# A hybrid decoder trunk on one core: the attention outputs are turned inside the next job, and the plan dates combined rows later

## The chip, the core and the metric

The kernel runs on one core of one Trainium2 chip. A core has TensorE (matrix multiplies, called PE in the profile; its weight loads are PEld), VectorE (DVE), ScalarE (ACT), GpSimd (POOL) and SyncE (SP, which here only issues transfers). TensorE writes to PSUM, which has eight banks; the other engines copy results from there to SBUF. The metric is the device time of one execution in microseconds (us); less is better.

## The reference

Two layers of a decoder trunk over one sequence of 2048 positions, width 1024. Each layer computes

```
h = rmsnorm(x); proj = h @ w_in
o_mla  = softmax attention, 6 heads, q/k of 96, v of 64
o_diff = 4 heads: p = softmax(s0) - lam * softmax(s1); o = rmsnorm(p @ v)
o_rw   = RWKV-7 recurrence, 6 heads of 64
x = x + concat(o_mla, o_diff, o_rw) * silu(gate) @ w_out
```

and a final RMSNorm closes the trunk. Both attentions are causal. The second is called the difference attention below: its weights are the difference of two softmaxes, so two rows of exponentials are combined into one before the values are applied. All is float32.

## The kernel before

**Stages.** In each of the two layers the input projections and the RWKV recurrence come first (phase A), then both attentions side by side, then the output projection (`outp`). The first attention, `mla`, starts as soon as the projections are done, the difference attention, `diff`, when the recurrence is done; `outp` waits for the flag `diff` and, tile by tile, for the flag `mla`.

**Jobs.** An attention works through jobs of one head and 256 queries (two blocks of 128 queries, `qi` 0 and 1); `g` counts them from 0 to 7, and a job with a larger `g` has more keys, up to 2048. `mla` has 48 jobs a layer and `diff` 32. A score chain makes the rows of a job: matmuls of queries and keys into PSUM (line 1128), a pass of VectorE that masks, keeps a running extreme in `mx` and empties the bank (L1131), and one exponential of ScalarE on each 1024 columns (L1139). In `diff` this is done twice, into tiles `row` and `tmp`, and then `row + cf * tmp` is formed in pieces of 512 columns (`CPART`), each either on VectorE (one instruction, L1429) or on GpSimd (two, L1431 and L1432). A value chain, in the function `weighted` (lines 1052 to 1087), then turns the rows: TensorE transposes up to four blocks of 128 columns into one bank (L1064), ScalarE or VectorE copies the bank back over the row (L1066), matmuls with the values add up the output (L1074), the output is copied to `ob` (L1082), and `ob` is turned back (L1086). What follows is the finish of a job: a multiplication by the reciprocal of the softmax sum into `ot` (L1323, L1475), in `diff` also a norm (ScalarE L1480, VectorE and GpSimd L272 and L273, GpSimd L1483), and a transfer to `omt` in DRAM (L1324, L1485).

**The order.** Python generators, one for each chain, are interleaved by `weave` on a clock of planned times, `clk`. A chain yields the time from which it can go on; `weave` takes the chain that is ready, with a handicap for each chain (`BIAS_A`, `BIAS_D`, `BIAS_M`, `BIAS_O`). When none is ready the planned clock moves on to the earliest. The order in which the chains emit matmuls and transposes is the order of TensorE's instructions on the chip, which are run strictly in that order: a plan that dates something too early puts an instruction into the queue that then waits, with all behind it. The time at which a tile of a row is ready is kept in `row.done`, one number for each 1024 columns. A combination in `diff` sets it from `clk.best`, which chooses the engine from two linear costs and reserves that engine:

```
eng, t = clk.best(max(ready, clk.now), V=65 + 1.04 * n, P=PX + 3.25 * n)   # PX = -700
rr[0].done[c0 // 1024] = max(rr[0].done[c0 // 1024], t)
```

**Limits on running ahead.** The score chain may be `JA` = 4 jobs ahead of `done["n"]`, which the value chain counts up when a job is finished, and it needs free row tiles: 8 of 1024 columns in `mla`, 9 in `diff` with 4 of `tmp`. A row tile is free again when the value matmuls have read it (`row.read`).

Of the kernel before, what the change touches and what calls it, by code (L numbers as in the profile page):

```python
# [15 lines left out]
ALU = mybir.AluOpType  # L16
# [7 lines left out]
NT = S // 128  # L24
# [5 lines left out]
MH, MN, MR, MV = 6, 64, 32, 64  # L30
MQ = MN + MR
QR, KVR = 256, 128
DH, DD, DV = 4, 32, 64
# [20 lines left out]
DROWS, DTMP = 9, 4  # L54
JA = 4
PX = -700
HOP = 100.0
LOAD = 2500.0
VDB = 2
# [27 lines left out]
class Clock:  # L87
# [22 lines left out]
    def fit(self, t, eng, ns):  # L110

        i = self.taken[eng] = [x for x in self.taken.get(eng, []) if x[1] > self.now]
        t += HOP
        for s_, e in i:
# [5 lines left out]
    def run(self, t, eng, ns):  # L120

        t = self.fit(t, eng, ns)
        self.taken[eng] = sorted(self.taken[eng] + [(t, t + ns)])
        return t + ns + HOP

# [65 lines left out]
def trunk(tc, a, out):  # L191
    nc = tc.nc
    V, A, P, T, Q = nc.vector, nc.scalar, nc.gpsimd, nc.tensor, nc.sync
# [5 lines left out]
    def mk(p, shape, tag, dt=F32, bufs=None):  # L199
        return p.tile(list(shape), dt, name=tag, tag=tag, bufs=bufs)  # L200
# [70 lines left out]
    def rstd_of(dst, ss, scale, eps):  # L271
        V.tensor_scalar(dst, ss, scale, eps, ALU.mult, ALU.add)  # L272
        P.tensor_tensor(dst, dst, mhalf.to_broadcast(list(dst.shape)), ALU.pow)  # L273
# [20 lines left out]
    def phase_a(l, rq_t, near, far, flags):  # L294
# [380 lines left out]
        def rwkv_inv(u, cks):  # L675
# [10 lines left out]
            for s in range(1, SB - 1):  # L686
# [4 lines left out]
                V.tensor_tensor(w[:, 0:s, s + 1:SB], w[:, 0:s, s + 1:SB], t, ALU.add)  # L691
                te = clk.run(clk.run(te, "V", 65 + IPAD + 1.04 * n * m) - HOP, "V", 65 + IPAD + 1.04 * n * m) - HOP
                if s % 2 == 0:
# [355 lines left out]
        return list(zip([run_chain(), chunk_chain(), prep_chain(), out_chain(), later_chain(), proj_chain()], BIAS_A))  # L1049


    def weighted(rows, vget, g, p):


        copied = 0.0
        for c_ in range(g // 2 + 1):
            for qi, row in enumerate(rows):
                n = min(4, 2 * g + qi + 1 - 4 * c_)
                if n <= 0:
                    continue  # L1060
                yield from banks.wait(att, 1, lambda: row.done[c_ // 2])
                tp, b = banks.get(att, [128, 512])
                for k in range(n):
                    T.transpose(tp[:, k * 128:(k + 1) * 128], row.at(512 * c_ + 128 * k, 128), ident)  # L1064
                eng, t = clk.best(clk.pe(109 * n), A=50 + 0.84 * 128 * n, V=65 + 1.04 * 128 * n)
                (V.tensor_copy if eng == "V" else A.copy)(row.at(512 * c_, 128 * n), tp[:, 0:128 * n])  # L1066
                copied = max(copied, banks.give(b, t))
                yield clk.now
        yield from banks.wait(att, 1, lambda: copied)
        o, bo = banks.get(att, [128, 128])  # L1070
        for kb in range(2 * g + 2):
            for qi, row in enumerate(rows):
                if kb <= 2 * g + qi:
                    T.matmul(o[HEADS[qi]], vget(kb), row.at(kb * 128, 128), start=(kb == 0), stop=(kb == 2 * g + qi))  # L1074
                    clk.pe(108)
        clk.pe(250)
        for row in rows:
            for h in range(len(row.tiles)):
                row.read(h)
        ob = mk(p, [128, 128], "ob", bufs=2)  # L1080
        eng, t = clk.best(clk.now, A=158, V=198)
        (V.tensor_copy if eng == "V" else A.copy)(ob, o)  # L1082
        banks.give(bo, t)
        yield from banks.wait(att, 1, lambda: t)
        ps, b = banks.get(att, [128, 2, 64])
        T.transpose(ps.rearrange("p a b -> p (a b)"), ob, ident)  # L1086
        clk.pe(109)
        return ps, b
# [53 lines left out]
    def mla(l, rq_t, side, flags):  # L1142
# [3 lines left out]
        jobs, done = [], dict(n=0)  # L1146
# [164 lines left out]
                    jobs.append((hd, g, rows, lsum, vts))  # L1311

        def value_chain():
            for n in range(MH * NT // 2):
                yield lambda: len(jobs) > n
                hd, g, rows, lsum, vts = jobs[n]
                li = mk(tp_, [128, 2], "li")
                if g >= 4:
                    V.tensor_tensor(lsum[:, :, 0], lsum[:, :, 0], lsum[:, :, 1], ALU.add)
                V.reciprocal(li, lsum[:, :, 0])  # L1320
                ps, b = yield from weighted(rows, lambda kb: vts[kb // 4][:, kb % 4, hd % 2], g, tp_)
                t = mk(tp_, [128, 2, 64], "ot", bufs=4)
                V.tensor_tensor(t, ps, li.unsqueeze(2).to_broadcast([128, 2, 64]), ALU.mult)  # L1323
                Q.dma_start(out=sc["omt"][g * 256:(g + 1) * 256, hd * MV:(hd + 1) * MV].rearrange("(q p) c -> p q c", p=128),  # L1324
                            in_=t)
                done["n"] = flags["mla"] = n + 1
                yield banks.give(b, clk.run(clk.now, "V", 200))
            st.close()

        return list(zip([value_chain(), score_chain()], BIAS_M))  # L1330

    def diff(l, side, flags):
# [3 lines left out]
        jobs, done = [], dict(n=0)  # L1336
# [61 lines left out]
        def scores(h, g, qt, kts):  # L1398
            nonlocal dist
            rows = []  # L1400
            lsum = mk(tp_, [128, 2, 2, 2], "dls", bufs=JA + 2)
            for qi in range(2):
                i = 2 * g + qi
                nk = 128 * (i + 1)
                rr = []
                now, dist = dist, distances((i + 1) % NT, l + h == 0 and i + 1 < NT)
                yield now[1]
                for m in range(2):
                    def passes(c_, n):
                        return [(qt[:, m, qi * 128:qi * 128 + 128], kts[c_][:, m, 0:n])]  # L1410

                    def sub(c_, n, nc_):
                        return now[0][c_ // 2][:, 512 * (c_ % 2):512 * (c_ % 2) + n]

                    rr.append((yield from attend_qk(new[m], tp_, DSN, i, passes, sub, SLOPES[h], lsum[:, m, qi])))
                if nk > 1024:
                    V.tensor_tensor(lsum[:, :, qi, 0], lsum[:, :, qi, 0], lsum[:, :, qi, 1], ALU.add)
                cf = mk(tp_, [128, 1], "cf", bufs=4)
                V.reciprocal(cf, lsum[:, 1, qi, 0:1])
                V.scalar_tensor_tensor(cf, cf, nlam[:, 0:1], lsum[:, 0, qi, 0:1], ALU.mult, ALU.mult)  # L1420
                ready = clk.run(rr[1].done[-1], "V", 210)
                for k in range(len(rr[0].tiles)):
                    rr[0].done[k] = 0.0
                for c0 in range(0, nk, CPART):
                    n = min(nk - c0, CPART)
                    p, q = rr[0].at(c0, n), rr[1].at(c0, n)
                    eng, t = clk.best(max(ready, clk.now), V=65 + 1.04 * n, P=PX + 3.25 * n)
                    if eng == "V":
                        V.scalar_tensor_tensor(p, q, cf[:, 0:1], p, ALU.mult, ALU.add)  # L1429
                    else:  # L1430
                        P.tensor_scalar(q, q, cf[:, 0:1], 1.0, ALU.mult, ALU.mult)  # L1431
                        P.tensor_tensor(p, p, q, ALU.add)  # L1432
                    rr[0].done[c0 // 1024] = max(rr[0].done[c0 // 1024], t)
                for k in range(len(rr[1].tiles)):
                    rr[1].read(k)
                rows.append(rr[0])
            return rows, lsum
# [27 lines left out]
                    jobs.append((h, g, rows, lsum, vts))  # L1465

        def value_chain():
            for n in range(DH * NT // 2):
                yield lambda: len(jobs) > n
                h, g, rows, lsum, vts = jobs[n]  # L1470
                li = mk(tp_, [128, 2], "dli")
                V.reciprocal(li, lsum[:, 0, :, 0])
                ps, b = yield from weighted(rows, lambda kb: vts[kb // 4][:, kb % 4], g, tp_)
                t = mk(tp_, [128, 2, 64], "ot", bufs=4)
                V.tensor_tensor(t, ps, li.unsqueeze(2).to_broadcast([128, 2, 64]), ALU.mult)  # L1475
                free = banks.give(b, clk.run(clk.now, "V", 200))
                r = mk(tp_, [128, 2], "r", bufs=4)
                for qi in range(2):
                    sq = mk(tp_, [128, DV], "sq")
                    A.activation(sq, t[:, qi], AF.Square, accum_out=r[:, qi:qi + 1])  # L1480
                clk.run(free, "A", 480)
                rstd_of(r, r, 1.0 / DV, SUB_EPS)
                P.tensor_tensor(t, t, r.unsqueeze(2).to_broadcast([128, 2, 64]), ALU.mult)  # L1483
                c0 = MH * MV + h * DV
                Q.dma_start(out=sc["omt"][g * 256:(g + 1) * 256, c0:c0 + DV].rearrange("(q p) c -> p q c", p=128), in_=t)  # L1485
                done["n"] = n + 1
                yield free
            st.close()
            flags["diff"] = 1

# [97 lines left out]
    with tc.manual_schedule(engines={mybir.EngineType.PE}):  # L1588
        for l in range(L):
            near, far = "left", "right"  # L1590
            flags = dict(near=0, far=0, diff=0, mla=0)
# [24 lines left out]
```

## Time and profile before

| | us |
|---|---|
| time, median of 3 runs | 4140.12 (4137.6 to 4142.48) |
| the profiled execution | 4140.24 |
| its span, first to last instruction | 4138.5 |
| first attention stage with both attentions | about 1180 to 1870 |
| second one | about 3250 to 3910 |

The profile page gives the busy time of each engine. Matmuls are pipelined, so that a busy TensorE isn't one at its peak. A view of groups gives for each line its count, busy time, mean duration, and behind the second bar the idle time of the engine just before the group's instructions with what ended it. A view of waits lists who waited for what, in total, how often, and the longest. The timeline shows single stretches; behind a row, in brackets, is the idle time before it and what ended it. The granted clock of TensorE has two levels in these records: 1.00 is 2.4 GHz and 0.50 is 1.2 GHz.

### The profile page before, as it was taken

The page shows a single profiled execution, that of the slowest core. Times are in us where ns is not written, and L with a number is a line of the kernel's source. Part 1 is how long each engine was busy: PE and PEld are TensorE (multiplying, and loading weights), DVE is VectorE, ACT ScalarE, POOL GpSimd, SP SyncE. Part 2 cuts the span into 40 slices and gives each one's busy share as a digit, 9 for nine tenths or more (in the row PEclk, how much of TensorE's full clock was granted, in tenths as well). Part 3 has the DMA queues.
Part 4 walks back from the last instruction along what each step waited for, and adds up shares of the span by engine and source line. Part 5 has one row for each costly group of instructions (what it writes and reads, how often), then busy time and mean ns, then how long its engine had stood idle before and what let it go on. Part 6 is the DMA issues. An engine that isn't in the chain of part 4 may idle for free. (4 is left out here: it accounts for less than half of the span.)

```text
span 4138.5 us, 76536 instructions
## 1 busy us (share of the span) xinstructions
PE 3634.2 (88%) x27232; PEld 2927.9 (71%) x27232; DVE 2777.0 (67%) x7443; ACT 1915.8 (46%) x4507; POOL 1447.4 (35%) x1684
## 2 busy tenths in 40 slices
PE   6989989898877888989999899998988789888699
PEld 5766767676666777777776676676766677777577
DVE  3775667756767888983237766677667678888633
ACT  3444344443456656751044444444434566666511
POOL 3434344443223334421044443444422243344211
PEclk9999999999989989999999999999989899999899
DMA  4533444344465554626434444343444555445254
GB/s 113 137 98 99 106 110 123 87 108 121 123 181 175 160 155 143 179 91 212 141 102 124 109 109 111 88 129 85 110 107 121 148 159 165 132 141 164 88 178 138
DMA packets 681630, 534.69 MB, mean 129 GB/s; under 512 B 233344, under 2 KB 585120, under 8 KB 681248
## 3 DMA queue, kind: packets, MB, share of 16 engines
q1 hardware_dynamic: 636704, 506.20, 44.1%
q10 hardware_dynamic: 40448, 11.02, 1.3%
q0 software_dynamic: 4096, 12.59, 0.9%
q8 instruction: 215, 3.52, 0.4%
q14 instruction: 167, 1.37, 0.1%
HBM read 417.43 MB, written 112.21 MB: 128 GB/s over the span
## 5 line engine op out<-in xcount | busy, mean ns | idle before, releaser
L441 PE MATMUL b<-h,wh 128*128 128x512 f32 x3584 | 1207.7, 412 | 51.9 <-DVE xk L470 15.8
L397 POOL TENSOR_TENSOR wl<-raw,wh 128x512 fp32r<-128x512 f32 x440 | 607.2, 1383 | 706.8 <-ACT wh L396 611.9
L441 PEld LDWEIGHTS b<-h,wh 128*128 128x128 f32 x3584 | 678.5, 193 | 220.9 <-DVE xk L470 18.8
L441 PE MATMUL b<-h,wl 128*128 128x512 f32 x1760 | 719.6, 409 | 2.6 <-POOL wl L397 2.5
L1139 ACT ACTIVATE row<-row,mx 128x1024 f32<-128x1024 f32 (+6 forms) x480 | 428.8, 895 | 245.0 <-DVE mx L1131 228.9
L396 ACT CAST wh<-raw 128x512 fp32r<-128x512 f32 x448 | 273.3, 613 | 505.8 <-PE b L441 310.6
L1064 PE MATMUL b<-ident,row 128*128 128x128 f32 x2720 | 389.9, 292 | 129.1 <-DVE row L1429 54.7
L1064 PEld LDWEIGHTS b<-ident,row 128*128 128x128 f32 x2720 | 329.7, 150 | 174.1 <-DVE row L1429 33.5
L441 PEld LDWEIGHTS b<-h,wl 128*128 128x128 f32 x1760 | 338.7, 192 | 79.4 <-POOL wl L397 5.8
L1128 PE MATMUL b<-k,q 128*128 128x512 f32 (+3 forms) x1440 | 369.3, 386 | 25.0 <-DVE mx L1131 16.5
L1128 PEld LDWEIGHTS b<-k,q 128*128 128x128 f32 x1440 | 252.0, 196 | 76.9 <-DVE mx L1131 23.7
L689 DVE TENSOR_TENSOR am<-w 48x30 f32<-48x30 f32 (+14 forms) x480 | 220.8, 460 | 88.6 <-DMA w<-linv 76.1
L1066 ACT COPY row<-b 128x512 f32<-128x512 f32 (+3 forms) x434 | 204.0, 505 | 111.3 <-PE b L1064 106.1
L1066 DVE COPY row<-b 128x512 f32<-128x512 f32 (+3 forms) x366 | 219.5, 621 | 49.6 <-PE b L1064 46.4
L1431 POOL TENSOR_SCALAR tmp<-tmp,cf 128x512 f32<-128x512 f32 (+2 forms) x144 | 118.4, 827 | 366.9 <-DVE cf L1420 238.1
L691 DVE TENSOR_TENSOR w<-w,am 48x30 f32<-48x30 f32 (+14 forms) x480 | 235.8, 491 | 12.9
L1074 PE MATMUL b<-row,v 128*64 128x128 f32 x3264 | 227.9, 287 | 13.2 <-ACT row L1066 7.7
L1074 PEld LDWEIGHTS b<-row,v 128*64 128x64 f32 x3264 | 202.1, 144 | 36.7 <-ACT row L1066 11.9
L1128 PE MATMUL b<-dk,dq 128*128 128x512 f32 (+3 forms) x640 | 200.6, 401 | 26.8 <-DVE mx L1131 12.3
L1564 PE MATMUL b<-wo,m 128*128 128x512 f32 x512 | 206.0, 402 | 0.0
L1139 ACT ACTIVATE tmp<-tmp,mx 128x1024 f32<-128x1024 f32 (+2 forms) x192 | 171.3, 894 | 73.9 <-DVE mx L1131 73.7
L1566 PE MATMUL b<-wo,m 128*128 128x512 f32 x512 | 203.5, 397 | 0.0
(279 smaller groups left out, 6629.7 us busy)
## 6 DMA issues: line engine op xcount, KB each, us to landing
raw<-in_w_in_dram SPq DMA_DIRECT2D x432, 256.0 KB
lq<-lat SPq DMA_DIRECT2D x192, 256.0 KB
d<-dist SPq DMA_DIRECT2D x70, 512.0 KB
lk<-lat SPq DMA_DIRECT2D x48, 512.0 KB
x<-in_x_dram SPq DMA_DIRECT2D x32, 512.0 KB
gat<-st SPq DMA_DIRECT2D x64, 256.0 KB
dk<-dqk SPq DMA_DIRECT2D x128, 128.0 KB
dq<-dqk SPq DMA_DIRECT2D x256, 64.0 KB
```

The lines of the kernel that those rows point to most:

```text
L396: A.copy(hi[:, :, 0:m], raw[:, :, 0:m])
L397: P.tensor_tensor(lo[:, :, 0:m], raw[:, :, 0:m], hi[:, :, 0:m].bitcast(F32), ALU.subtract)
L441: T.matmul(ps[0:w], x[k // 4][:, k % 4, 0:w], y, start=(k == 0 and i == 0), stop=(k == KD - 1 and i == len(ops) - 1))
L689: V.tensor_tensor(t, w[:, 0:s, s:s + 1].to_broadcast([48, n, m]), w[:, s:s + 1, s + 1:SB].to_broadcast([48, n, m]), ALU.mult)
L691: V.tensor_tensor(w[:, 0:s, s + 1:SB], w[:, 0:s, s + 1:SB], t, ALU.add)
L1064: T.transpose(tp[:, k * 128:(k + 1) * 128], row.at(512 * c_ + 128 * k, 128), ident)
L1066: (V.tensor_copy if eng == "V" else A.copy)(row.at(512 * c_, 128 * n), tp[:, 0:128 * n])
L1074: T.matmul(o[HEADS[qi]], vget(kb), row.at(kb * 128, 128), start=(kb == 0), stop=(kb == 2 * g + qi))
L1128: T.matmul(ps[:, 0:n], x, y, start=(i_ == 0), stop=(i_ == len(ops) - 1))
L1139: A.activation(row.at(1024 * h, n), row.at(1024 * h, n), AF.Exp, bias=mx0, scale=-1.0, accum_out=lsum[:, h:h + 1])
L1564: T.matmul(ps, m[0][:, k], wo[0][:, k, hs], start=(k == 0), stop=False)
L1566: T.matmul(ps, m[1][:, k], wo[0][:, k, hs], start=False, stop=(k == KD - 1))
```

## The change

It has two parts. In the first, `weighted` ends at the copy to `ob` and returns it; the turning back of `ob` and all of the finish become a generator, `finish`, which is handed to the next job as `late` and runs there behind the turning of that job's rows and ahead of its value matmuls; the last job's runs behind the loop. `done["n"]` is counted up without waiting for it, while the flag `mla` stays in the finish. `li` and `dli` get a third buffer. In the second part, the planned time at which a combined piece is there (`row.done`) is moved back by 0.83 ns for each column on VectorE and 2.85 ns on GpSimd; the choice of the engine and the time reserved on it stay.

```diff
+VLATE, PLATE = 0.83, 2.85
-    def weighted(rows, vget, g, p):
+    def weighted(rows, vget, g, p, late):
@@ weighted, behind the loop that turns the rows
                 yield clk.now
+        yield from late()
         yield from banks.wait(att, 1, lambda: copied)
@@ weighted, behind the value matmuls
         (V.tensor_copy if eng == "V" else A.copy)(ob, o)
         banks.give(bo, t)
+        return ob, t
+
+    def by_query(ob, t):
+
         yield from banks.wait(att, 1, lambda: t)
         ps, b = banks.get(att, [128, 2, 64])
         T.transpose(ps.rearrange("p a b -> p (a b)"), ob, ident)
@@ mla, value_chain
+            def finish(n, hd, g, li, ob, t):
+                ps, b = yield from by_query(ob, t)
                 t = mk(tp_, [128, 2, 64], "ot", bufs=4)
                 V.tensor_tensor(t, ps, li.unsqueeze(2).to_broadcast([128, 2, 64]), ALU.mult)
...
-                done["n"] = flags["mla"] = n + 1
+                flags["mla"] = n + 1
                 yield banks.give(b, clk.run(clk.now, "V", 200))
+            late = lambda: iter(())
+            for n in range(MH * NT // 2):
+                yield lambda: len(jobs) > n
+                hd, g, rows, lsum, vts = jobs[n]
+                li = mk(tp_, [128, 2], "li", bufs=3)
...
+                ob, t = yield from weighted(rows, lambda kb: vts[kb // 4][:, kb % 4, hd % 2], g, tp_, late)
+                late = lambda n=n, hd=hd, g=g, li=li, ob=ob, t=t: finish(n, hd, g, li, ob, t)
+                done["n"] = n + 1
+            yield from late()
@@ diff, scores: the combination
                     if eng == "V":
                         V.scalar_tensor_tensor(p, q, cf[:, 0:1], p, ALU.mult, ALU.add)
+                        t += VLATE * n
                     else:
                         P.tensor_scalar(q, q, cf[:, 0:1], 1.0, ALU.mult, ALU.mult)
                         P.tensor_tensor(p, p, q, ALU.add)
+                        t += PLATE * n
                     rr[0].done[c0 // 1024] = max(rr[0].done[c0 // 1024], t)
@@ diff, value_chain: finish and late in the same way as in mla
```

## Rows read from the trace of the kernel before

**Rows 1.** The page, busy time of each engine, share of the span, instructions.
```profile
PE 3634.2 (88%) x27232; PEld 2927.9 (71%) x27232; DVE 2777.0 (67%) x7443; ACT 1915.8 (46%) x4507; POOL 1447.4 (35%) x1684
```

**Rows 2.** Windows, both attention stages: from:to, length, busy us (instructions), PEclk, DMA.
```profile
1180.00:1870.00 690.00, 585.72 (x4901) 495.77 (x4896) 562.97 (x1699) 426.83 (x1044) 244.45 (x325) 0.93 0.54 158
...
3250.00:3910.00 660.00, 570.50 (x4895) 488.16 (x4891) 538.53 (x1667) 407.52 (x1023) 239.32 (x304) 0.95 0.49 139
```

**Rows 3.** Waits of TensorE, whole span: who for whom: us in total, times, longest.
```profile
PE b L1064 <- DVE row L1429: 54.7, 23, 5.9
...
PE b L1128 <- DVE mx L1131: 28.8, 40, 1.8
PE b L1064 <- DVE mx L1131: 21.7, 26, 2.2
PE b L1064 <- POOL row L1432: 19.8, 12, 5.3
...
PE b L1243 <- DVE mx L1131: 7.3, 10, 1.8
PE b L1086 <- ACT ob L1082: 7.3, 6, 3.4
...
PE b L1086 <- DVE ob L1082: 7.0, 5, 3.2
```

**Rows 4.** Groups of instructions by shape, whole span: combinations and `ob` copies.
```profile
L1429 DVE SCALAR_TENSOR_TENSOR row<-tmp,cf,row 128x512 f32<-128x512 f32 x152 | 155.2, 1046 | 1.7
L1432 POOL TENSOR_TENSOR row<-row,tmp 128x512 f32<-128x512 f32 x72 | 99.2, 1378 | 2.3
...
L1431 POOL TENSOR_SCALAR tmp<-tmp,cf 128x512 f32<-128x512 f32 x72 | 70.2, 975 | 258.9 <-DVE cf L1420 168.0 <-DVE r L272 18.5 <-ACT sq L1480 16.0
...
L1082 ACT COPY ob<-b 128x128 f32<-128x128 f32 x100 | 26.0, 260 | 133.0 <-PE b L1074 132.8
...
L1082 DVE COPY ob<-b 128x128 f32<-128x128 f32 x60 | 17.1, 286 | 23.8 <-PE b L1074 23.5
```

**Rows 5.** Timeline 1752 to 1768: start, us, engine, line, what [idle before].
```profile
1758.44 4.31 DVE L1429 SCALAR_TENSOR_TENSOR row<-tmp,cf,row 128x512 f32<-128x512 f32 x2
...
1762.67 0.28 DVE L1082 COPY ob<-b 128x128 f32<-128x128 f32 x1
...
1763.00 0.33 PE L1086 MATMUL b<-ident,ob 128*128 128x128 f32 x1 [3.16 <-DVE ob L1082]
```

**Rows 6.** Timeline 1510 to 1530: a combined row that TensorE waits for.
```profile
1521.09 2.42 DVE L1429 SCALAR_TENSOR_TENSOR row<-tmp,cf,row 128x512 f32<-128x512 f32 x3
...
1521.89 1.97 PE L1064 MATMUL b<-ident,row 128*128 128x128 f32 x8 [2.33 <-DVE row L1429]
...
1525.93 4.32 PE L1064 MATMUL b<-ident,row 128*128 128x128 f32 x19 [2.07 <-POOL row L1432]
```

**Rows 7.** Windows behind such waits; after ACT and POOL comes PEclk.
```profile
1228.20:1231.60 3.40, 3.26 (x13) 2.59 (x14) 3.40 (x12) 1.70 (x7) 2.37 (x3) 0.51 0.85 321
1313.60:1320.40 6.80, 6.33 (x27) 5.82 (x28) 5.43 (x16) 5.98 (x17) 5.47 (x8) 0.50 0.99 340
...
3740.50:3743.90 3.40, 3.40 (x18) 3.40 (x17) 3.07 (x4) 1.36 (x5) 2.37 (x3) 0.50 0.17 34
1852.90:1856.30 3.40, 3.35 (x16) 3.35 (x17) 2.37 (x3) 1.45 (x3) 0.00 (x0) 0.50 0.76 205
```

**Rows 8.** Timeline, the ends of the first and of the second attention stage.
```profile
1847.10 0.38 SPq L1485 DMA_DIRECT2D omt<-ot  x1
...
1852.95 0.47 PE L1086 MATMUL b<-ident,ob 128*128 128x128 f32 x1 [3.35 <-ACT ob L1082]
...
1858.20 3.71 PE L1074 MATMUL b<-row,v 128*64 128x128 f32 x62
1867.93 1.30 PE L1538 MATMUL b<-ident,io 128*128 128x128 f32 x5 [6.01 <-DMA io<-omt]
...
1870.50 0.38 SPq L1324 DMA_DIRECT2D omt<-ot  x1
...
3911.23 0.37 SPq L1485 DMA_DIRECT2D omt<-ot  x1
...
3936.53 1.30 PE L1538 MATMUL b<-ident,io 128*128 128x128 f32 x5 [27.73 <-DMA io<-omt]
```

More of the change, by code (lines that the diff above doesn't have):

```diff
@@ L1313, in value_chain @@
         def value_chain():
[L1314 to L1321, printed above, removed]
+            def finish(n, hd, g, li, ob, t):
+                ps, b = yield from by_query(ob, t)
                 t = mk(tp_, [128, 2, 64], "ot", bufs=4)
@@ L1325, in value_chain @@
                             in_=t)
-                done["n"] = flags["mla"] = n + 1
+                flags["mla"] = n + 1
                 yield banks.give(b, clk.run(clk.now, "V", 200))
+            late = lambda: iter(())
[3 more added lines that the diff above has]
+                li = mk(tp_, [128, 2], "li", bufs=3)
+                if g >= 4:
+                    V.tensor_tensor(lsum[:, :, 0], lsum[:, :, 0], lsum[:, :, 1], ALU.add)
+                V.reciprocal(li, lsum[:, :, 0])
+                ob, t = yield from weighted(rows, lambda kb: vts[kb // 4][:, kb % 4, hd % 2], g, tp_, late)
+                late = lambda n=n, hd=hd, g=g, li=li, ob=ob, t=t: finish(n, hd, g, li, ob, t)
+                done["n"] = n + 1
+            yield from late()
             st.close()
@@ L1467, in value_chain, with finish @@
         def value_chain():
[L1468 to L1473, printed above, removed]
+            def finish(h, g, li, ob, t):
+                ps, b = yield from by_query(ob, t)
                 t = mk(tp_, [128, 2, 64], "ot", bufs=4)
@@ L1485, in value_chain @@
                 Q.dma_start(out=sc["omt"][g * 256:(g + 1) * 256, c0:c0 + DV].rearrange("(q p) c -> p q c", p=128), in_=t)
+                yield free
+            late = lambda: iter(())
+            for n in range(DH * NT // 2):
+                yield lambda: len(jobs) > n
+                h, g, rows, lsum, vts = jobs[n]
+                li = mk(tp_, [128, 2], "dli", bufs=3)
+                V.reciprocal(li, lsum[:, 0, :, 0])
+                ob, t = yield from weighted(rows, lambda kb: vts[kb // 4][:, kb % 4], g, tp_, late)
+                late = lambda h=h, g=g, li=li, ob=ob, t=t: finish(h, g, li, ob, t)
                 done["n"] = n + 1
-                yield free
+            yield from late()
             st.close()
```

## The prediction

> **What bounds the kernel now.** I read the page first: TensorE is busy 88% of the span, VectorE 67% [rows 1]. The change touches only the stages in which the attentions run, so I read those two windows next: TensorE is busy 585.72 of 690 us and 570.50 of 660 us (85 and 86%), VectorE 562.97 and 538.53 (82% of each) [rows 2]. Neither is full. TensorE's queue is in order, so its idle time is the price of instructions that were put ahead of their data. The list of waits says which ones [rows 3]: turning a combined row waits 54.7 us for VectorE's combination (23 times, mean 2.38) and 19.8 us for GpSimd's (12 times, mean 1.65); turning `ob` back waits 7.3 + 7.0 = 14.3 us for the copy; and scores, queries and row turnings wait 28.8 + 21.7 + 7.3 = 57.8 us, in 76 short waits, for VectorE to empty a PSUM bank (`mx`). The first two kinds are what the change aims at, 88.8 us together; the third kind stays and is what would be late next.
>
> A long wait costs more than itself. Behind some of them the granted clock is 0.50, that is 1.2 GHz, for 3.4 us or twice that, while TensorE is almost fully busy [rows 7]. I find three such stretches behind waits for `ob` (first 1228.2, last 1852.9; each 3.4 us) and nine behind waits for a combined row (first 1313.6, last 3740.5; together 55 us). Work done there at full speed would take half: 5 us and some 27 us.
>
> **Part one, `ob` turned in the next job.** It removes no instruction. Per job it moves one transpose of TensorE, one multiplication of VectorE, in `diff` also two squares of ScalarE, a small VectorE and two GpSimd instructions, and SP's transfer to `omt`, past the next job's row turnings. The copy itself takes only 260 or 286 ns [rows 4]; the waits come from what is queued ahead of it. At 1758.44 two combinations hold VectorE for 4.31 us, the `ob` copy behind them starts at 1762.67, and TensorE stands for 3.16 us [rows 5]. At 1852.95 it stands 3.35 us [rows 8]. With the change the next job's turnings and their copies lie between copy and transpose, and that is the cover: the value matmuls come behind in any case. If that cover is gone (the last job of each attention has none), the wait is as before. Nothing new waits: `omt` is read only by `outp`; the moved GpSimd and ScalarE instructions go behind a few row copies and combinations, and nobody waits for them before the stage's end; SP's loads for later jobs no longer stand behind this transfer, whose source is ready earlier relative to its place. `done["n"]` counts up sooner, which lets scores start sooner but not in larger number, since row tiles limit them for large `g`. I take the whole wait as gone: 14.3 + 5 = 19 us, with bounds of 0 and 19, since one transposition more ahead of the value matmuls can only displace work and adds none.
>
> **Part two, the later date.** Planned, a piece of 512 columns takes 65 + 1.04 x 512 = 597 ns on VectorE and -700 + 3.25 x 512 = 964 ns on GpSimd. The trace has 1046 and 975 + 1378 = 2353 ns [rows 4]. The change adds 425 and 1459 ns, to 1022 and 2423: the dates become those of the trace. It moves a turning only where the plan arrives earlier than that. Where it does, the chain yields and another chain's matmuls go ahead, so that the wait shrinks by the delay. On all 23 + 12 waits of [rows 3] that makes 23 x 0.425 + 12 x 1.459 = 9.8 + 17.5 = 27.3 us. One number holds for both pieces of a 1024-column tile, so a GpSimd neighbour moves VectorE's pieces too; were all 35 moved by 1.459, it would be 51. If no other chain is ready at those points, the plan only idles, the order stays, and it is 0. I take 27.3, the value that needs no assumption on neighbours. It doesn't cure the waits: [rows 6] shows 2.33 and then 2.07 us in one job, where three combinations in a row took 2.42 us and GpSimd's piece came later still; the reserved time on VectorE stays too short, so pieces behind one another add up their error. Of the 27 us at half clock I take a third, 9 us, because a wait of 2.4 us shortened to 1 us often has no such stretch behind it, and those of 3 to 6 us keep it. Part two: 36 us, bounds 0 and 78.
>
> The mean in [rows 4] hides a spread, and here a rule speaks against part two. In [rows 5] two combinations that run beside GpSimd take 4.31 us, twice the mean of 1.05 each. The Trainium skill (SBUF — State Buffer, section "SBUF: two separate sides") says that GpSimd and VectorE hold a shared pair of ports exclusively, so that an instruction of VectorE with two SBUF inputs stands while a GpSimd one has it. By that rule a fixed delay for each column dates the undisturbed pieces and not the ones that TensorE waits for; the VectorE share of the sum, 9.8 us, would be 0 and the time about 5 us later than forecast. The trace agrees on the disturbance, by that 4.31 us; whether the rule decides the waits no row says.
>
> **What is given back.** Gross 19 + 36 = 55 us. The other side is VectorE: its work is unchanged, 1101.5 us in 1350 us of the two stages [rows 2]; in 1295 us it would be busy 85% instead of 82%, and waits for `mx` grow with that. They are already 57.8 us at 82%. I let half of the gross come back as such waits: 55 / 2 = 27.5. The profiled execution took 4140.24, the median is 4140.12, so they can be taken as one: 4140.2 - 27.5 = 4112.7, say 4112 us. With both parts at their bounds and half given back the sum goes from 4140 (nothing) to 4140 - (19 + 78) / 2 = 4092; 4043 would need all of it and nothing given back.
>
> **The rivals.**
>
> First, VectorE takes it all: the matmuls that move ahead of a late row are scores, each of which needs a bank that VectorE must empty, and VectorE is just then busy with the combinations. For it: `mx` is the second largest cause today [rows 3]. Against it: VectorE still idles 18% of the stage [rows 2], and value matmuls of the other attention need no VectorE. Or, with the same result, part two doesn't do what it says, because the waiting rows are late by VectorE's queue and not by their duration; then only part one is left and half of that comes back. Time 4140 - 10 to 4140, say 4135.
>
> Second, slower: the difference attention falls behind. Its value chain is held up in the plan by up to 1.46 us in each job that waits (35 waits, some 9 jobs a layer, 13 us a layer), and the first attention goes ahead in the gaps. In the first layer the difference attention now ends first: its last transfer is at 1847.10, that of `mla` at 1870.50, and the loads of `w_out` that start when it is done are hidden but for 6.01 us by the last `mla` jobs. In the second layer it ends last, at 3911.23, and the same loads cost 27.73 us of an idle TensorE [rows 8]. If it came last in both layers, the first would pay 27.7 - 6.0 = 22 us more and the second up to 13. It decides from a delay of about 11 us on, half of the 23 us by which it is ahead in layer one. With 19 / 2 = 10 us of part one kept: 4140 + 22 + 13 - 10 = 4165 at the most; 4155 with half the second layer's delay lost to other work.
>
> Third, more (and the way towards that 4043): once a chain yields, what slips in is a whole block. A job's value matmuls go out in one piece of 3.71 us [rows 8], longer than the mean wait, and so can fill it wholly. Then 88.8 us of waits and 32 us of half clock are open; with half given back 4140 - 60 = 4080.
>
> **How the numbers follow.** Forecast 4112, own range 4092 to 4130: 0.50. VectorE takes it, or part two misses (4135, 4132 to 4148): 0.20. The difference attention falls behind (4155, 4149 to 4165): 0.13. Whole blocks fill (4080, 4043 to 4092): 0.17. A measurement of this kernel tells 0.2%, 8 us, from no change. Faster by more: 0.50 + 0.17 = 0.67; within: 0.20; slower: 0.13. The range that leaves out the far half of the third rival and of the slower one, somewhat under 2 in 10, is 4068 to 4152.
>
> **What would show it.** In the changed kernel, waits of L1086 for `ob` should be below 2 us in all, and none of 3 us. Waits of L1064 for L1429 and L1432 should go from 74.5 to 35 to 50 us. Waits for `mx` should rise from 57.8 to 70 to 85 us: if they rise by more than 50, the first rival is right. The last `omt` transfers of the two attentions show the second: if that of the difference attention is the later one in both layers, with 28 us of idle TensorE ahead of the first L1538 in each. The forecast is wrong if waits for combined rows stay where they are or if other waits of a row (L1066, L1139) grow by tens of us.

## The result, and the profile after

The changed kernel takes 4091.24 us (median of 4 runs, 4090.18 to 4097.99) against 4139.15 for the kernel before beside it (4137.6 to 4142.48). The ratio is 0.989, 95% interval 0.9874 to 0.9905: 48 us less, where 28 were forecast. The profiled execution took 4091.09 us, its span is 4089.0.

The page of the changed kernel, the line of busy times (engine, busy us, share of the span, instructions):

```profile
PE 3606.5 (88%) x27232; PEld 2902.1 (71%) x27232; DVE 2754.5 (67%) x7414; ACT 1932.5 (47%) x4538; POOL 1445.1 (35%) x1680
```

TensorE has the same number of instructions as in [rows 1] and is busy 27.7 us less with them. So not all of the gain is idle time: part of the same work ran faster. The waits of TensorE in the changed kernel say what happened to the idle time (who waits for whom, us in total, times, longest; the lines have moved: row turnings are L1065, the turning of `ob` L1092, scores L1134, the pass of VectorE that fills `mx` L1137, queries L1249, combinations L1442 on VectorE and L1446 on GpSimd, the first step of the output projection L1559):

```profile
PE b L1559 <- DMA io<-omt: 61.3, 4, 27.5
...
PE b L1065 <- DVE mx L1137: 23.8, 31, 4.4
...
PE b L1065 <- DVE row L1442: 21.6, 9, 5.1
...
PE b L1134 <- DVE mx L1137: 16.7, 27, 2.6
...
PE b L1092 <- DVE mx L1137: 9.5, 8, 2.5
PE b L1092 <- ACT row L1067: 8.4, 6, 2.0
...
PE b L1065 <- POOL row L1446: 6.4, 8, 2.3
...
PE b L1249 <- DVE mx L1137: 1.7, 2, 1.3
```

Against [rows 3], the waits for combined rows went from 54.7 to 21.6 us (VectorE's pieces) and from 19.8 to 6.4 (GpSimd's). Scores wait 16.7 instead of 28.8 for VectorE to empty a bank. The waits of the `ob` turning for its copy, 7.3 + 7.0, are no longer among these rows; but two new ones are, 9.5 + 8.4, of the same instruction. The groups by shape show them in one row each (idle time of the engine just before, and what ended most of it behind the second bar):

```profile
L1442 DVE SCALAR_TENSOR_TENSOR row<-tmp,cf,row 128x512 f32<-128x512 f32 x153 | 147.5, 989 | 1.6
L1446 POOL TENSOR_TENSOR row<-row,tmp 128x512 f32<-128x512 f32 x71 | 102.1, 1438 | 2.5
...
L1092 PE MATMUL b<-ident,ob 128*128 128x128 f32 x160 | 46.0, 293 | 19.7 <-DVE mx L1137 9.5 <-ACT row L1067 8.4 <-ACT ob L1084 0.7
```

The combinations cost what they did in [rows 4] (989 and 1438 ns against 1046 and 1378). The `ob` turning stands 19.7 us in all. It reads neither `mx` nor a row: what it waits for is the PSUM bank that it writes, which a pass of VectorE or a row copy of ScalarE must first empty. In the kernel before, the same view has:

```profile
L1086 PE MATMUL b<-ident,ob 128*128 128x128 f32 x160 | 42.6, 283 | 15.3 <-ACT ob L1082 7.3 <-DVE ob L1082 7.0 <-ACT kr L1206 0.5
```

So the wait has another name and is no smaller, 19.7 us against 15.3. Then the price of the new order, TensorE's timeline at the end of the first attention stage (start, us, engine, line, what; in brackets the idle time before, and what ended it):

```profile
1793.44 1.97 PE L1065 MATMUL b<-ident,row 128*128 128x128 f32 x8 [5.03 <-DVE row L1442]
...
1810.17 1.94 PE L1065 MATMUL b<-ident,row 128*128 128x128 f32 x8 [5.12 <-DVE row L1442]
...
1819.22 0.33 PE L1092 MATMUL b<-ident,ob 128*128 128x128 f32 x1 [0.36 <-ACT ob L1084]
1845.96 1.30 PE L1559 MATMUL b<-ident,io 128*128 128x128 f32 x5 [26.41 <-DMA io<-omt]
```

and the last transfers of the two attentions on SP's queue in that stretch, L1324 of `mla` and L1496 of `diff`:

```profile
1784.21 0.37 SPq L1324 DMA_DIRECT2D omt<-ot  x1
...
1822.06 0.38 SPq L1496 DMA_DIRECT2D omt<-ot  x1
```

In [rows 8] the difference attention was done 23 us ahead of `mla`, and TensorE stood 6.01 us for the output projection's first tile. Now it is done 38 us behind, alone for its last jobs, and TensorE stands 26.41. Two waits of 5.03 and 5.12 us, nearly half of what is left for VectorE's pieces, lie behind the last transfer of `mla`, where only the difference attention's own chains are left to put something in. In the second layer the difference attention is last as before (27.50 us against 27.73).

**One account of it all.** I take the two attention stages, each from the last projection matmul to the first matmul of the output projection, and split their length by TensorE's records: idle time by the instruction that waits and by what ended it; the wait for the output projection's first tiles; a surcharge, which is half of the busy time inside stretches of granted clock 0.50; and the rest, work at full clock. The parts add up to the stages' length within 1.2 us. The wait for the first tiles is one row of the view of waits, 61.3 us in the list above; the kernel before has:

```profile
PE b L1538 <- DMA io<-omt: 40.8, 4, 27.7
```

| us, both layers | before | after | difference |
|---|---|---|---|
| row turnings, for a combined row | 74.5 | 28.0 | -46.5 |
| row turnings, for anything else | 53.4 | 69.1 | +15.7 |
| `ob` turnings, for the copy | 14.3 | 1.3 | -13.0 |
| `ob` turnings, for a bank or anything else | 0.9 | 17.9 | +17.0 |
| value matmuls | 14.5 | 9.3 | -5.2 |
| scores, queries and the rest | 91.5 | 78.9 | -12.6 |
| surcharge of half clock | 95.4 | 63.4 | -32.0 |
| wait for the output projection's first tiles | 40.8 | 61.3 | +20.5 |
| work at full clock | 1344.4 | 1345.1 | +0.7 |
| both stages | 1730.8 | 1675.3 | -55.5 |

The whole span is 49.5 us shorter (4138.5 to 4089.0), so outside of these stages 6 us are lost again: 8.0 more from the first output projection to the end of the second layer's projections, 2 less elsewhere.

### The profile page after: what moved, and what is told of

It is laid out like the page before. It is cut to its first block, busy times and chain, and to the rows that moved or that the text cites. A ratio compares the mean times of both kernels' runs of the same rounds, so it can differ in the third digit from the quotient of the medians.

```text
span 4089.0 us, 76505 instructions
## 1 busy us (share of the span) xinstructions
PE 3606.5 (88%) x27232; PEld 2902.1 (71%) x27232; DVE 2754.5 (67%) x7414; ACT 1932.5 (47%) x4538; POOL 1445.1 (35%) x1680
## 3 DMA queue, kind: packets, MB, share of 16 engines
q0 software_dynamic: 4096, 12.59, 0.9%
q8 instruction: 215, 3.52, 0.4%
## 5 line engine op out<-in xcount | busy, mean ns | idle before, releaser
L1145 ACT ACTIVATE row<-row,mx 128x1024 f32<-128x1024 f32 (+7 forms) x480 | 428.9, 896 | 197.5 <-DVE mx L1137 190.6
L1065 PE MATMUL b<-ident,row 128*128 128x128 f32 x2720 | 392.3, 285 | 97.6 <-DVE mx L1137 23.8
L1065 PEld LDWEIGHTS b<-ident,row 128*128 128x128 f32 x2720 | 320.9, 146 | 150.9 <-DVE mx L1137 34.9
L1134 PE MATMUL b<-k,q 128*128 128x512 f32 (+3 forms) x1440 | 378.8, 387 | 23.4 <-DVE mx L1137 11.5
L1134 PEld LDWEIGHTS b<-k,q 128*128 128x128 f32 x1440 | 247.4, 194 | 72.9 <-DVE mx L1137 14.2
L1067 ACT COPY row<-b 128x512 f32<-128x512 f32 (+3 forms) x460 | 222.9, 519 | 121.0 <-PE b L1065 108.1
L1445 POOL TENSOR_SCALAR tmp<-tmp,cf 128x512 f32<-128x512 f32 (+3 forms) x142 | 115.7, 820 | 392.1 <-DVE cf L1433 226.9
L692 DVE TENSOR_TENSOR w<-w,am 48x30 f32<-48x30 f32 (+14 forms) x480 | 227.0, 473 | 12.7
L1134 PE MATMUL b<-dk,dq 128*128 128x512 f32 (+3 forms) x640 | 198.9, 397 | 26.3 <-ACT row L1067 7.3
L1067 DVE COPY row<-b 128x512 f32<-128x512 f32 (+3 forms) x340 | 199.3, 602 | 25.0 <-PE b L1065 23.5
L1585 PE MATMUL b<-wo,m 128*128 128x512 f32 x512 | 205.9, 402 | 0.0
L1587 PE MATMUL b<-wo,m 128*128 128x512 f32 x512 | 203.3, 397 | 0.0
L1586 PE MATMUL b<-wo,m 128*128 128x512 f32 x512 | 203.2, 397 | 0.0
```

Of the source, the lines that this page charges most:

```text
L1134: T.matmul(ps[:, 0:n], x, y, start=(i_ == 0), stop=(i_ == len(ops) - 1))
L1145: A.activation(row.at(1024 * h, n), row.at(1024 * h, n), AF.Exp, bias=mx0, scale=-1.0, accum_out=lsum[:, h:h + 1])
L1585: T.matmul(ps, m[0][:, k], wo[0][:, k, hs], start=(k == 0), stop=False)
L1586: T.matmul(ps, m[0][:, k], wo[1][:, k, hs], start=False, stop=False)
L1587: T.matmul(ps, m[1][:, k], wo[0][:, k, hs], start=False, stop=(k == KD - 1))
```

## The experiments

Two readings were open. In the first, the forecast's own, both parts take waits away, each for its reason, and the difference attention's late end gives some of it back. In the second, every edit to the plan's dates or order interleaves all of the work anew, and the times of two orders differ by as much as the gain, whatever the edit was for. The first five runs do one part alone, change one part, or change a handicap of the plan; the last seven change nothing but a constant that belongs to neither part.

### Part one alone

```diff
-VLATE, PLATE = 0.83, 2.85
+VLATE, PLATE = 0.0, 0.0
```

> The changed kernel with both added dates at 0, so that part one (the finish inside the next job) stands alone. Theory, parts add up: waits of TensorE for ob nearly gone as in the changed kernel, waits for combined rows as before (74.5 us), time 4110 to 4122. Rival, part one carries the whole gain because the value chain no longer stands behind each output copy: 4085 to 4098, with waits for combined rows falling although nothing in this kernel dates them later. Rival, luck of the interleaving: any time between 4085 and 4145 with no tie to the waits.

Measured: 4134.52 us (10 runs, 4122.01 to 4144.98), ratio 0.9989 [0.9975, 1.0002], not to be told from no change, and above the 4110 to 4122 of the theory. The waits of TensorE in this kernel:

```profile
PE b L1065 <- DVE row L1442: 53.4, 25, 5.1
...
PE b L1065 <- DVE mx L1137: 29.8, 36, 3.0
...
PE b L1559 <- DMA io<-omt: 60.5, 4, 27.5
```

and the group of its `ob` turnings:

```profile
L1092 PE MATMUL b<-ident,ob 128*128 128x128 f32 x160 | 46.5, 297 | 12.8 <-ACT row L1067 6.5 <-DVE mx L1137 4.8 <-ACT ob L1084 1.1
```

The waits for the copy are gone (1.1 us), those for a bank have come (6.5 + 4.8), and the instruction stands 12.8 us where it stood 15.3. Combined rows are waited for as before (53.4 against 54.7 for VectorE's). In this kernel too the difference attention ends last in the first layer, and the waits for the output projection's first tiles are 60.5 us instead of 40.8, which takes back 20 us of what it gains elsewhere. (The profiled execution, 4122.44 us, is one of the two shortest of the ten.)

### Part two alone

The finish goes back behind the job's own value matmuls; the dates stay.

```diff
-    def weighted(rows, vget, g, p, late):
+    def weighted(rows, vget, g, p):
...
-        yield from late()
...
-        return ob, t
-
-    def by_query(ob, t):
```

> The kernel before with the added dates of 0.83 and 2.85 ns a column, so that part two stands alone. Theory, parts add up: waits for combined rows fall from 74.5 to 30 to 45 us, waits for ob stay at about 14 us, time 4108 to 4122. Rival, part one carries the whole gain: 4132 to 4145, and the waits for combined rows move elsewhere (to the emptying of banks, or to the end of the stage).

Measured: 4115.55 us (4 runs, 4111.9 to 4117.0), ratio 0.9942 [0.9924, 0.9961]. Its waits:

```profile
PE b L1065 <- DVE mx L1132: 37.0, 45, 2.9
...
PE b L1065 <- DVE row L1430: 25.5, 9, 6.4
...
PE b L1087 <- ACT ob L1083: 3.8, 6, 1.8
...
PE b L1087 <- DVE ob L1083: 1.9, 3, 0.9
```

Waits for VectorE's pieces fall to 25.5 us, close to the 21.6 with both parts, and GpSimd's to 12.0. But the waits for the copy to `ob` fall as well, from 14.3 to 5.7 us, though nothing about them was changed. And the two parts alone make 4.6 + 23.6 = 28 us together, where the change has 48. Both fit a new order that does something on its own, though for the sum an interplay of the two parts would do as well.

### The finish ahead of the next job's row turnings

It is still in the next job, but without the cover of the row turnings.

```diff
+        yield from late()
         for c_ in range(g // 2 + 1):
...
-        yield from late()
         yield from banks.wait(att, 1, lambda: copied)
```

> The changed kernel with the finish of the job before put ahead of the turning of the next job's rows instead of behind it, so that its only cover is what the plan puts between two jobs. Theory (the row turnings are the cover of the output copy): waits for ob come back in part, 5 to 12 us, and the time is 10 to 25 us above the changed kernel (4101 to 4116). Rival (any place in the next job does): within 8 us of the changed kernel, waits for ob below 3 us.

Measured: 4072.5 us (4 runs, 4067.67 to 4078.33), ratio 0.9836 [0.9813, 0.9858]. I had expected 4101 to 4116, and it is faster than the change itself. Its waits:

```profile
PE b L1066 <- DVE row L1442: 14.4, 5, 6.1
...
PE b L1092 <- ACT ob L1084: 6.9, 6, 3.9
...
PE b L1092 <- DVE ob L1084: 4.7, 5, 1.6
```

The waits for the copy are back, 11.6 us in these two rows, as expected; the waits for a bank are gone with them (1.3 us), and all `ob` turnings stand 13.0 us. In these two orders the cover does what it was made for and is worth nothing at this instruction: with it the sum is 19.7 us, without it 13.0. What is better than in the changed kernel stands elsewhere, at the second layer's end, in the timeline of TensorE:

```profile
1859.41 1.30 PE L1559 MATMUL b<-ident,io 128*128 128x128 f32 x5 [27.65 <-DMA io<-omt]
...
3875.16 0.74 PE L1559 MATMUL b<-ident,io 128*128 128x128 f32 x5 [3.98 <-DMA io<-omt]
```

and in the last transfers of the two attentions in that layer:

```profile
3853.80 0.37 SPq L1496 DMA_DIRECT2D omt<-ot  x1
...
3876.93 0.43 SPq L1324 DMA_DIRECT2D omt<-ot  x1
```

Here `mla` came last in the second layer, and 3.98 us are paid in place of 27.50.

### The dates moved twice as far

```diff
-VLATE, PLATE = 0.83, 2.85
+VLATE, PLATE = 1.66, 5.70
```

> The changed kernel with the added dates doubled, 1.66 and 5.70 ns a column. Theory (the dates were still too early, since pieces on VectorE queue behind one another): waits for combined rows fall below those of the changed kernel (28 us) to 10 to 20 us, time 4080 to 4090. Rival (the difference attention falls behind): the first attention ends earlier still against it, the idle stretch ahead of the first output projection stays at 26 to 28 us in both layers or grows, and the time is 4095 to 4115.

Measured: 4083.03 us (4 runs, 4081.68 to 4090.82), ratio 0.9869 [0.9849, 0.9889]: the time that was expected, but not for the reason. Its waits:

```profile
PE b L1065 <- DVE row L1442: 31.9, 11, 7.6
```

Waits for GpSimd's pieces fall to 0.4 us; those for VectorE's are 31.9, where 10 to 20 were expected. In this run the larger delay takes the waits for GpSimd's pieces away and leaves those for VectorE's.

### The difference attention favoured in the plan

It was to end first again in the first layer.

```diff
-BIAS_D = 750, 5250
+BIAS_D = 1500, 7000
```

> The changed kernel with the handicap of the difference attention's chains raised from 750 and 5250 to 1500 and 7000, so that the plan lets it end about 20 us ahead of the first attention in both layers. Theory (the order in which the attentions end costs the changed kernel some 26 us in each layer, as idle TensorE while w_out is loaded): the stretch from the last omt transfer to the first output projection falls from 30 and 31 us to 4 to 10 in both layers, and the time to 4040 to 4060. Rival (the idle stretch only moves, because the first attention's last jobs then run alone and wait for themselves): tails short but the attention stage longer by as much, time 4080 to 4095.

Measured: 4088.13 us (4 runs, 4084.78 to 4092.07), ratio 0.988 [0.9863, 0.9896], no different from the changed kernel, and not the 4040 to 4060 of the theory. Transfers on SP's queue, and the first tile on TensorE, in the timeline of the first layer's end, and the first tile of the second layer:

```profile
1807.44 0.36 SPq L1496 DMA_DIRECT2D omt<-ot  x1
...
1813.09 0.38 SPq L1496 DMA_DIRECT2D omt<-ot  x1
...
1834.21 0.48 SPq L1324 DMA_DIRECT2D omt<-ot  x1
...
1838.85 1.30 PE L1559 MATMUL b<-ident,io 128*128 128x128 f32 x5 [6.94 <-DMA io<-omt]
...
3881.31 1.30 PE L1559 MATMUL b<-ident,io 128*128 128x128 f32 x5 [14.43 <-DMA io<-omt]
```

In the first layer it did end first, 21 us ahead of `mla`, and the first tile costs 6.94 us again, in the second layer 14.43; the waits for first tiles are 28.1 us in all instead of 61.3. But waits for combined rows rise by 19.8 us to 47.7, those of scores and the rest by 10.8, and the two stages together are only 11 us shorter (1664.1 against 1675.3). The price of the late end is real, and whoever saves it by a new order draws the other waits anew.

### The same kernels in other orders

`HOP` is what the plan adds for each passage from one engine to another. It belongs to no part of the change, and TensorE's instructions stay the same 27232; but dates shift by some ns, ties fall the other way, and the order comes out different. The plan also gives some copies and combinations to another engine (VectorE has 7419 to 7443 instructions in the five kernels before). Both kernels with 96, 98 and 102, and the kernel before with 104:

```diff
-HOP = 100.0
+HOP = 98.0     # or 96.0, 102.0, 104.0
```

With 98, the changed kernel and the kernel before:

> The changed kernel with one constant of the plan that belongs to no part of the change (the 100 ns that the plan adds for a hop between engines) at 98, which only shuffles the interleaving. Theory (the gain is in the attention stages and the tails are luck): both attention stages together, without tails, 1600 to 1630 us (changed kernel 1615, before 1696), time 4065 to 4110 by how the tails fall. Rival (the whole gain is luck of the interleaving): 1660 to 1700 us without tails, time 4120 to 4145.

> The kernel before with the same shuffle (98). In its plan the difference attention ends first in both layers. Theory: both attention stages without tails 1680 to 1710 us, the tail of the second layer short, time 4110 to 4140. Rival (luck): anything from 1600 to 1700 us, time 4080 to 4140.

With 102:

> As the run with 98, with 102. Theory: both attention stages without tails 1600 to 1630 us, time 4065 to 4110. Rival: 1660 to 1700 us, time 4120 to 4145.

> The kernel before with the plan's hop constant at 102. So far shuffles of the kernel before gave 4139 (100) and 4099 us (98), of the changed kernel 4091 (100), 4123 (98) and 4100 us (102). Theory (the change has an effect of its own beside the shuffle): the kernel before lies in the upper part, 4115 to 4145 us, with waits for ob of 10 to 15 us in any shuffle. Rival (shuffle alone): 4085 to 4115 us.

With 96, and 104 for the kernel before:

> The changed kernel with the constant at 96. Theory: the mean of the changed kernel's four shuffles lies at least 15 us below that of the kernel before, so this one at 4080 to 4110 us; waits for ob below 6 us. Rival (shuffle alone): no tie, 4085 to 4145 us.

> The kernel before with the constant at 96. Theory: 4115 to 4145 us. Rival (shuffle alone): 4085 to 4115 us.

> The kernel before with the constant at 104. Theory: 4115 to 4145 us. Rival (shuffle alone): 4085 to 4115 us.

Measured, medians of 2 to 8 runs in us, with the ratio to the kernel before at 100:

| `HOP` | kernel before | changed kernel | difference |
|---|---|---|---|
| 96 | 4138.52, 1.0003 [0.9985, 1.0022] | 4070.85, 0.9838 [0.9808, 0.9868] | -68 |
| 98 | 4098.93, 0.9903 [0.9883, 0.9923] | 4122.93, 0.9962 [0.995, 0.9973] | +24 |
| 100 | 4139.15 | 4091.24, 0.989 [0.9874, 0.9905] | -48 |
| 102 | 4156.0, 1.005 [1.0036, 1.0064] | 4100.23, 0.9906 [0.9886, 0.9926] | -56 |
| 104 | 4150.87, 1.0037 [1.002, 1.0054] | | |

A constant that has nothing to do with the change makes the kernel before 40 us faster at 98, nearly as much as the change does, and at that value the change makes it 24 us slower. The kernel before has a mean of 4137 over its five orders with a standard deviation of 22, the changed kernel 4096 over its four, again with 22. The difference of the means is 40 us with a standard error of 15, which with so few orders is an interval of some 6 to 75. So both readings hold in part: the change very likely has an effect of its own, of a size that nine orders leave wide open, and any one pair of orders gives it with an error of some 30 us. The misses were of that sort: the kernel before at 98 (4110 to 4140 expected), and at 102 and 104, above what was expected; the changed kernel at 96, below the 4080 to 4110 expected; and the changed kernel at 98, whose 4122.93 us lie above the 4065 to 4110 of the theory and in the 4120 to 4145 of the rival, by which the whole gain is luck. Taken alone that run would have decided against the change.

The waits of the kernel before at 98 show where a good part of its 40 us comes from:

```profile
PE b L1064 <- DVE row L1429: 15.6, 11, 3.4
...
PE b L1064 <- POOL row L1432: 12.6, 12, 1.9
...
PE b L1086 <- ACT ob L1082: 12.1, 12, 3.3
```

and those of the changed kernel at 98:

```profile
PE b L1065 <- DVE row L1442: 37.5, 20, 8.4
```

The 54.7 us that the prediction started from are 15.6 in another order of the same kernel; and 37.5 are possible with the later dates. The account of above, as means over the orders, shows which parts belong to the change and which to the draw (ranges in brackets):

| us, both layers | before, 5 orders | after, 4 orders | difference |
|---|---|---|---|
| combined rows, VectorE's pieces | 35 (16 to 55) | 23 (15 to 38) | -11 |
| combined rows, GpSimd's pieces | 17 (11 to 24) | 8 (4.5 to 13) | -9 |
| row turnings, for anything else | 60 (47 to 83) | 61 (51 to 69) | +1 |
| all of the `ob` turnings | 13.5 (9 to 16) | 16.4 (8 to 24) | +3 |
| of these, for the copy | 11.7 (8 to 14) | 2.0 (0.7 to 5) | -10 |
| value matmuls | 18 (11 to 26) | 13 (8 to 21) | -5 |
| scores and queries, for `mx` | 40 (36 to 43) | 17 (14 to 20) | -23 |
| all else | 56 (48 to 69) | 64 (59 to 73) | +8 |
| surcharge of half clock | 77 (59 to 95) | 64 (60 to 71) | -13 |
| wait for the output projection's first tiles | 48 (34 to 63) | 56 (47 to 64) | +8 |
| work at full clock | 1346 (1339 to 1353) | 1340 (1332 to 1345) | -6 |

The differences add up to -47 in the stages. Three rows of waits are worth naming. Two have ranges that don't touch: the waits of `ob` turnings for the copy, which came back under another name (what the same turnings wait for a bank is 1 to 3 us before and 8 to 19 after), and the waits of scores and queries for `mx`, 23 us less. The latter fall in every kernel that has the finish in the next job (21.3 with part one alone, 20.2 with doubled dates, 23.8 with the difference attention favoured, 23.5 with the finish ahead of the row turnings), and less with part two alone (30.2). So part one seems to do its work there and not at `ob`. Some of it only moves to other instructions: counted at all of TensorE's instructions in the two stages, waits for `mx` are 69 us in the mean of the kernels before (63 to 77) and 53 in that of the changed ones (48 to 58), 16 us less; they are 56.3 with part one alone, 69.6 with part two alone, and 64.0 with the finish ahead of the row turnings. Why they fall, no run shows: `done["n"]` is counted up a finish earlier, and a bank is asked for at another place, and neither was tried alone. The third is GpSimd's pieces, whose ranges overlap a little (11 to 24 and 4.5 to 13). The doubled dates bring them to 0.4, below any other run, which speaks for part two; but part one alone has 11.7 and part two alone 12.0, so at the dates of the change the runs don't show it.

Three of the versions are faster than the kernel before and the changed one: the changed kernel with `HOP` 96 (4070.85), the finish ahead of the turnings (4072.5) and the doubled dates (4083.03). With a scatter of 22 us between orders none of the three shows a better idea; they are good orders.

## Why the prediction was right, and where it was wrong

**The sign and the wide range**, 4068 to 4152, were right, and the forecast of 4112 was 21 us too high: the time lies just below the forecast's own 4092 to 4130, at the edge of the third rival's range. The mean effect over orders is the less certain 40 us, 12 more than the 28 forecast, well inside its interval. That the forecast came near is less than it seems: it argued from the waits of one order, and with a scatter of 22 us on each side a right sum could have come out 30 us off. Nor do its terms come out one by one. In the account of the pair, what the two parts aimed at brings 46.5 + 13.0 + 32.0 = 91.5 us where the sum had 55, and 15.7 + 17.0 + 20.5 = 53 us come back where the sum had 27.5, at places other than the one that it named.

**Part one, 14.3 us of waits: the failed step.** "Nothing new waits" was wrong. Its first half held: the waits for `ob` went to 1.3 us, under the 2 that I had named, and none is of 3 us. But the turning needs a PSUM bank, and now it asks for one right behind the row turnings, which have just taken theirs. The same instruction waits 17.9 us for banks (9.5 for passes of scores and 8.4 for row copies that must empty one), and its sum went up by 4.0 us. I had looked at what the instruction reads and not at what it writes. The finish ahead of the turnings is the test: copy waits back, bank waits gone, and the sum no larger. Over all 14 kernels it is the same: the waits for a bank are 8 to 19 us in the seven that have the finish behind the row turnings, and 0.5 to 3 in the others.

**Part two, 27.3 us of waits.** In this pair 46.5, within the bounds of 0 and 51 that the prediction had for it, but the waits that stay, 28.0 us, are below its sign of 35 to 50; over the orders about 20. The size was read from an order with more of these waits than the four others (74.5 against 28.2 to 65.1). For GpSimd's pieces the kind of mechanism may be right (17 to 8 over the orders, and 0.4 doubled). Of VectorE's pieces the forecast itself said that errors add up along the queue, and they are what stays: 54.7 to 21.6 us in this pair, over the orders 35 to 23 with ranges that overlap, and 31.9 with the doubled dates.

The traces tell how these pieces are late. Of the 54.7 us of the kernel before, 33.4 pass before the combination that TensorE waits for has begun, and in 17 of the 23 waits it then takes 739 to 752 ns, less than its mean of 1046. The longest wait (the combination on VectorE, and the turning behind it):

```profile
3287.09 0.74 DVE L1429 SCALAR_TENSOR_TENSOR row<-tmp,cf,row 128x512 f32<-128x512 f32 x1
...
3287.89 1.75 PE L1064 MATMUL b<-ident,row 128*128 128x128 f32 x7 [5.90 <-DVE row L1429]
```

In the changed kernel it is 15.2 of 21.6 us, with doubled dates 21.7 of 31.9, over the nine orders 152 of 267. So these pieces mostly start late; they don't mostly take long, and a delay that is sized by a piece's duration isn't made for that. This is what the prediction's first rival said in its second half (late by VectorE's queue and not by their duration), and what the sum for VectorE's share had wrong. The Trainium skill (SBUF — State Buffer, section "SBUF: two separate sides") says that VectorE and GpSimd hold their shared ports exclusively, from which I had made another reason for a price of 0. The trace agrees that GpSimd disturbs: in the kernel before, the 75 combinations that ran more than 0.8 us beside GpSimd took 1326 ns in the mean, the 77 others 774. But it isn't the disturbed pieces that TensorE mostly waits for.

One wait of the changed kernel shows such a late start (the timeline, ScalarE, VectorE and GpSimd):

```profile
1807.36 1.13 ACT L1145 ACTIVATE tmp<-tmp,mx 128x1024 f32<-128x1024 f32 x1
...
1809.27 3.52 DVE L1442 SCALAR_TENSOR_TENSOR row<-tmp,cf,row 128x512 f32<-128x512 f32 x3
1809.41 1.17 POOL L1445 TENSOR_SCALAR tmp<-tmp,cf 128x512 f32<-128x512 f32 x1 [6.59 <-DVE cf L1433]
```

TensorE stood 5.12 us until 1810.17. For most of it the combination had not begun: its factor `cf` needs the last exponential of ScalarE, which ends at 1808.49. The three pieces then take 3.52 us beside GpSimd, 1.17 each.

**Half clock, 5 + 9 us.** In this pair 32.0, over the orders 13. I had found 32 us behind the waits and took a third of the share behind combined rows; the account has 95.4 in the stages, three times what I had found. The 27.7 us less of busy time on the page fit that. Over the nine orders the surcharge goes with the waits for combined rows, from 59 us at 28 us of waits to 95.4 at 74.5, close to a line of 0.67 us for each us (correlation 0.97); part two alone, with 37.5 us of waits and 81 of surcharge, lies off it. No run changes one without the other, so that the one causes the other is not shown; if it does, such a wait costs more than half as much again as its length. The stretches that stay stand where long waits stay, in the windows behind the two of 5 us, and TensorE's idle time ahead of the output projection is one of its own (from:to, length, busy us and instructions of PE, PEld, DVE, ACT and POOL, granted clock, DMA share, GB/s):

```profile
1824.00:1845.00 21.00, 0.00 (x0) 0.00 (x0) 8.72 (x8) 7.80 (x8) 0.00 (x0) 0.50 0.67 228
1793.40:1796.80 3.40, 2.66 (x11) 2.26 (x12) 3.26 (x6) 1.37 (x4) 3.34 (x4) 0.50 0.03 9
1810.10:1813.50 3.40, 3.14 (x14) 2.77 (x15) 2.70 (x2) 1.17 (x2) 2.06 (x2) 0.51 0.00 0
```

**Half given back as waits for `mx`: wrong in sign.** They were to rise from 57.8 to between 70 and 85. The same three rows are now 23.8 + 16.7 + 1.7 = 42.2, and 51.7 with the 9.5 of the `ob` turning; over the orders they fall too. The first half of the first rival (VectorE takes it all) falls with it. In the account of the pair, what is given back instead is 15.7 us of other waits of row turnings and 17.0 of `ob` turnings for banks.

**The second rival's mechanism came, without its sign.** The difference attention ends last in both layers, at 20.5 us in waits for first tiles where I had priced 22. I gave the case 0.13 as a slower kernel; it came beside a gain that was larger than I had summed. And it is a property of the order more than of the change: over the orders these waits are 48 against 56 us.

**The third rival**, whole value blocks in the gaps, can't be told apart: the time lies in its range of 4043 to 4092, by less than 1 us, and 11 us from its 4080; but the mean over orders, 4096, doesn't, and no view shows which block went where for which reason.

## What to carry to other kernels

A wait that moves away from an instruction's input can come back at its output: ask which buffer or bank the moved instruction takes, and what was put just ahead of it. And where the order of all work comes out of a plan, one pair of timings is a draw: time each version with a few values of a constant that shouldn't matter (here 2% of `HOP` made the kernel before 1% faster) before an edit is given its credit, and trust those rows of the account whose ranges don't touch.

## What the runs showed of the hardware

The same instructions of the two stages take 1332 to 1353 us of TensorE at full clock in the nine orders of the table; what an order costs beyond that is idle time (188 to 251 us), half clock (59 to 95) and the ends of the stages (34 to 64). That the work at full clock stays within 2% while the half clock varies from 59 to 95 us speaks for pricing half clock at half of the busy time in it. I had not expected it to be that large a part: in the profile of before it is 95.4 us, more than the 88.8 us of waits that the change was aimed at.
